# Making the low halves of streamed weights on VectorE instead of GpSimd

## The chip, the cores and the metric

The kernel runs on one core of a Trainium2 chip. A core has five engines that work side by side, each through its own queue in order: TensorE (PE; its weight loads are listed as PEld), VectorE (DVE), ScalarE (ACT), GpSimd (POOL) and SyncE (SP), which here issues the DMA transfers. The metric is the device time of one execution in microseconds (us); of several executions the median is given.

## The reference

One step of a decoder layer. A prompt of 2048 tokens and a small batch of 64 sample rows go through the same layer, of width 1024. In short:

```python
mod = jnp.einsum('bd,de->be', jax.nn.silu(c), w_ada) + b_ada     # six shifts, scales and gates
h = rms_norm(x, norm1_g) * (1 + sc1) + sh1
z = jnp.einsum('bld,de->ble', h, w_in)
q, k, v, g, u, gate_r, gate_s = jnp.split(z, IN_SPLITS, axis=-1)
ret = retention(rotary(q), rotary(k), v)     # then normalized, times silu(g)
ssm = s5(u, ...)                             # a complex diagonal scan, gelu, gated by w_glu
merged = sigmoid(gate_r) * (ret @ w_br) + sigmoid(gate_s) * (ssm @ w_bs)
x = x + gt1 * (merged @ w_out)
h2 = rms_norm(x, norm2_g) * (1 + sc2) + sh2
x = x + gt2 * (jnp.square(jax.nn.relu(h2 @ w_up)) @ w_down)
```

The outputs are the normalized rows of prompt and sample and the new states of both branches. All numbers are float32.

## The kernel before

The prompt is worked in four blocks of 512 tokens (`super_block`). After the four blocks comes one feed-forward stage (`feed_forward`) for all 2048 tokens, which has its own streams of weights and does not use the code of the change.

A float32 product is made of three products of a reduced type. Each operand is split: the high half is the value rounded to that type, the low half is what the rounding lost. PE then adds high times high, high times low and low times high in one PSUM bank (line 252, three matmuls per tile; 24 for one slice of weights against four banks).

The weights of the blocks come as one stream of slices of 128 x 2 x 512 numbers. The list of slices is laid down in `plan`: per block the matrices "u", "q", "k", "v", "g", four gate matrices, "glu", "br0", "br1", "bs0", "bs1", "wo0" and "wo1"; the first block also has eight matrices "ada4" to "ada11" of the modulation between them. The feed-forward of the 64 sample rows is worked on the side, with the matrices "us0" to "us7" in the third block and "ds0", "ds1" in the fourth, slice by slice between the others (`side`, line 226). There are 312 slices.

`fetch` (line 177) starts a slice's DMA into one of four raw buffers. `refill` (line 184) makes its two halves in one of five places of a ring: ACT rounds it into `whi` (line 190), and then the low half `wlo` is the difference of `wraw` and `whi` (line 193). After that the next fetch is issued; a fetch into a raw buffer waits on SP's queue until the low half of the slice that had it is made. A place of the ring comes free when PE has done its last product with it. In a block of the order "k" the refill for a used slice comes after the first bank's products of the next slice (lines 269 and 270); for "wo0" and "wo1" of the first three blocks, order "j", four refills come with the last bank.

What else uses the engines there: in the first block `s5_setup` (lines 933 to 1179) makes the tables of the scan, nearly all on DVE. In every block `s5` runs eight scan steps (lines 1206 to 1252), and `retention` four chunks (lines 1317 to 1359); both go back and forth between PE, DVE and ACT. DVE empties the banks of "q" and "k" (lines 1557 to 1559), of "v", "br", "bs" (lines 1699 and 1700) and "wo" (lines 1720 and 1721); ACT empties "u" and the gates. POOL makes further sums and low halves (lines 1347, 1560, 1649, 1702).

All these are generators that are stepped between groups of matmuls (`tick`), which lays down a program order. From this a planner, with its own assumed durations, sets the final order of each engine's queue ahead of time (line 1829); a tie to the program order is made where line 195 is called, for the first five slices. At run time every queue is worked in that fixed order.

Of the kernel before, what the change touches and what calls it, by code (L numbers as in the profile page):

```python
# [27 lines left out]
SIDE = ('us', 'ds')  # L28
# [53 lines left out]
class Layer:  # L82
# [101 lines left out]
    def refill(self, keep=False):  # L184
        nc = self.nc
        if self.split < len(self.stream):
            raw = self.rawq.pop(self.split)
            hi = self.ring.tile([P, 2, 512], F32R, name="whi")
            lo = self.ring.tile([P, 2, 512], F32R, name="wlo")
            a = nc.scalar.activation(hi, raw, AF.Copy)  # L190
            name = self.stream[self.split][0][:2]
            eng = nc.vector if name == "ad" or name in SIDE and self.split % 4 < 2 else nc.gpsimd
            l = eng.tensor_sub(lo, raw, hi)  # L193
            if keep:
                self.tc.keep_in_program_order(a)
                self.tc.keep_in_program_order(l)
            self.wq[self.split] = (hi, lo)
            self.split += 1
        self.fetch()
# [1641 lines left out]
```

## Time and profile before

| | |
|---|---|
| time, median of 3 runs (lowest to highest) | 3043.33 us (3043.03 to 3048.49) |
| the profiled execution | 3037.17 us |
| its span, first to last instruction | 3035.4 us |
| busy: PE, DVE, ACT, POOL | 2894.8, 1820.2, 1404.8, 1729.9 us |
| low halves made on POOL (line 193) | 248, busy 620.0 us |
| low halves made on DVE (line 193) | 64, busy 90.8 us |
| first and last low half start at | 40.7 and 1722.1 us |

In the profile's rows L193 is line 193 of the kernel, `wlo<-wraw,whi` says which tile is written from which, x248 is a count. In a list of groups, the numbers behind the bar are the busy time in us, the mean of one in ns, and the idle time of the engine just before them with what ended it. In a list of waits stand the waiting instruction, the one that ended the wait, the total in us, how often, and the longest. In a timeline the start in us and the duration come first; in the list of one source line the durations stand as shortest, median and longest in ns. PEclk is the share of TensorE's full clock that was granted.

### The profile page before, as it was taken

The numbers are of one execution on the slowest core, as the hardware profiler recorded it, in microseconds if no ns is written. First come the engines' busy times: TensorE is split into PE (matmuls) and PEld (weight loads), VectorE is DVE, ScalarE is ACT, GpSimd is POOL, SyncE is SP. The second block draws the span as 40 slices with busy tenths as digits, with TensorE's granted clock in tenths as the row PEclk, the third lists the DMA queues.
The fourth block names the chain that finished last, engine by engine and source line by source line (L and its number), as shares of the span: only waits on it lengthen the run. The fifth ranks groups of instructions, "written<-read, shape, count | busy, mean of one in ns | idle before, by whom it ended". The sixth has DMA issues, their size and how long they took to land.

```text
span 3035.4 us, 37377 instructions
## 1 busy us (share of the span) xinstructions
PE 2894.8 (95%) x13436; PEld 2371.7 (78%) x13436; DVE 1820.2 (60%) x2953; ACT 1404.8 (46%) x2280; POOL 1729.9 (57%) x1036
## 2 busy tenths in 40 slices
PE   8789999999999899999999999999999999999997
PEld 4568778788778788887788878887888788878886
DVE  6978544770676775365852655555556855555556
ACT  3223463322454334534344355555764555557743
POOL 3331355434354634565445677668777666679772
PEclk9889999999999999999999999999999999999998
DMA  8476435643236953447644555555544644457542
GB/s 264 140 210 196 131 128 175 184 119 119 82 100 211 280 172 114 144 161 229 191 132 146 179 179 185 185 200 203 180 160 160 211 167 153 154 203 248 190 153 98
DMA packets 337325, 518.62 MB, mean 171 GB/s; under 512 B 72038, under 2 KB 168822, under 8 KB 333035
## 3 DMA queue, kind: packets, MB, share of 16 engines
q1 hardware_dynamic: 337140, 516.24, 52.4%
q8 instruction: 106, 1.74, 0.2%
q14 instruction: 79, 0.65, 0.1%
HBM read 401.39 MB, written 114.78 MB: 170 GB/s over the span
## 4 chain that ended last, share of the span: by engine, by line
PE 75%; DVE 13%; DMA 4%; POOL 3%; ACT 2%; issue 2%; SPq 0%; ACTq 0%; DVEq 0%; POOLq 0%
PE pq_up L412 17%; PE pq_down L412 15%; PE pd_gr L252 6%; PE pd_wo L252 5%; PE pd_gs L252 5%; PE pd_br L252 3%; PE pd_u L252 2%; PE pd_g L252 2%; PE pd_bs L252 2%; PE pd_k L252 2%; PE pd_v L252 2%; PE pd_glu L252 2%; DMA sw<-sd 1%; POOL tw L310 1%; PE pd_q L252 1%
## 5 line engine op out<-in xcount | busy, mean ns | idle before, releaser
L193 POOL TENSOR_TENSOR wlo<-wraw,whi 128x1024 fp32r<-128x1024 f32 x248 | 620.0, 2512 | 701.0 <-ACT whi L190 582.9
L190 ACT ACTIVATE whi<-wraw 128x1024 fp32r<-128x1024 f32 x312 | 324.0, 1058 | 568.9 <-PE pd_wo L252 56.0
L412 PE MATMUL pq_down<-shi,tw 128*128 128x512 f32 x1792 | 561.1, 393 | 12.7 <-DVE acc L470 10.8
L412 PE MATMUL pq_up<-shi,tw 128*128 128x512 f32 x1776 | 552.6, 391 | 10.2 <-DVE tw L310 4.5
L412 PEld LDWEIGHTS pq_down<-shi,tw 128*128 128x128 f32 x1792 | 338.2, 189 | 85.4 <-ACT shi L399 7.9
L412 PEld LDWEIGHTS pq_up<-shi,tw 128*128 128x128 f32 x1776 | 334.6, 189 | 82.6 <-DVE tw L310 4.9
L310 POOL TENSOR_TENSOR tw<-traw,tw 128x512 fp32r<-128x512 f32 x191 | 280.5, 1482 | 150.9 <-ACT tw L309 150.5
L412 PE MATMUL pq_down<-slo,tw 128*128 128x512 f32 x896 | 351.0, 392 | 0.0
L412 PE MATMUL pq_up<-slo,tw 128*128 128x512 f32 x888 | 346.7, 391 | 0.0
L399 ACT ACTIVATE shi<-sw 128x1024 fp32r<-128x1024 f32 x140 | 146.9, 1057 | 159.3 <-DMA sw<-sd 109.6
L474 DVE SCALAR_TENSOR_TENSOR acc<-pq_down,modT,acc 128x512 f32<-128x512 f32 x224 | 161.7, 746 | 78.9 <-PE pq_down L412 78.5
L412 PEld LDWEIGHTS pq_down<-slo,tw 128*128 128x128 f32 x896 | 169.4, 189 | 34.4
L412 PEld LDWEIGHTS pq_up<-slo,tw 128*128 128x128 f32 x888 | 167.5, 189 | 34.5
L385 DVE TENSOR_TENSOR slo<-sw,far 128x512 fp32r<-128x512 f32 x160 | 104.2, 683 | 114.6 <-ACT far L384 102.8
L309 ACT ACTIVATE tw<-traw 128x512 fp32r<-128x512 f32 x223 | 136.7, 624 | 53.8 <-PE pq_down L412 37.3
L422 ACT ACTIVATE aq<-pq_up 128x512 f32<-128x512 f32 x128 | 72.5, 592 | 171.4 <-PE pq_up L412 171.4
L404 DVE TENSOR_TENSOR slo<-sw,shi 128x1024 fp32r<-128x1024 f32 x60 | 113.9, 1909 | 58.7 <-ACT shi L399 55.7
L193 DVE TENSOR_TENSOR wlo<-wraw,whi 128x1024 fp32r<-128x1024 f32 x64 | 90.8, 1421 | 72.2 <-ACT whi L190 67.7
L348 POOL TENSOR_TENSOR ts<-traw,ts 128x512 f32<-128x512 f32 x64 | 95.2, 1487 | 61.2 <-issue 51.2
L309 ACT ACTIVATE tw<-ts 128x512 fp32r<-128x512 f32 x127 | 79.5, 627 | 79.1 <-PE pq_up L412 72.2
L310 POOL TENSOR_TENSOR tw<-t,tw 128x512 fp32r<-128x512 f32 x64 | 88.1, 1385 | 35.3 <-ACT tw L309 35.3
L450 DVE TENSOR_TENSOR sq<-aq 128x512 f32<-128x512 f32 x32 | 29.6, 926 | 131.0 <-ACT aq L427 131.0
(546 smaller groups left out, 6939.8 us busy)
## 6 DMA issues: line engine op xcount, KB each, us to landing
wraw<-in_w_in_dram SPq DMA_DIRECT2D x144, 512.0 KB
sw<-sd SPq DMA_DIRECT2D x112, 512.0 KB
s5p<-s5c SPq DMA_DIRECT2D x32, 1024.0 KB
traw<-in_w_up_dram SPq DMA_DIRECT2D x64, 512.0 KB
sd<-sq SPq DMA_DIRECT2D x32, 1024.0 KB
sd<-aq SPq DMA_DIRECT2D x32, 768.0 KB
traw<-in_w_down_dram SPq DMA_DIRECT2D x24, 1024.0 KB
wraw<-in_w_ada_dram SPq DMA_DIRECT2D x32, 512.0 KB
```

The lines of the kernel that those rows point to most:

```text
L190: a = nc.scalar.activation(hi, raw, AF.Copy)
L193: l = eng.tensor_sub(lo, raw, hi)
L252: nc.tensor.matmul(banks[j], a, b, start=(k == 0 and z == 0), stop=(k == nk - 1 and z == 2))
L309: self.nc.scalar.activation(t[:, 0], x, AF.Copy)
L310: eng.tensor_sub(t[:, 1], x, t[:, 0])
L348: G.tensor_sub(x[p], l, x[m] if isinstance(m, int) else m)
L385: self.nc.vector.tensor_sub(d, a, c)
L399: nc.scalar.activation(hi[:, a], t, AF.Copy)
L404: V.tensor_sub(lo[:, a], t, hi[:, a])
L412: self.nc.tensor.matmul(bank, w, x, start=(first and a == 0 and z == 0), stop=(a == 3 and z == 2), skip_group_check=True)
L422: copy = lambda d, b: nc.scalar.activation(d, b, AF.Copy)
L474: V.scalar_tensor_tensor(d, b, g, d, op0=ALU.mult, op1=ALU.add)
```

## The change

Before, `refill` chose the engine of the subtraction by the name of the matrix: DVE for the "ada" matrices and for two of every four places of the side matrices "us" and "ds", POOL for all others. Now it is DVE for all 312. The subtraction's operands, the high half on ACT, the buffers and the fetches stay. The planner orders the queues anew.

```diff
             a = nc.scalar.activation(hi, raw, AF.Copy)
             name = self.stream[self.split][0][:2]
-            eng = nc.vector if name == "ad" or name in SIDE and self.split % 4 < 2 else nc.gpsimd
-            l = eng.tensor_sub(lo, raw, hi)
+            l = nc.vector.tensor_sub(lo, raw, hi)
             if keep:
                 self.tc.keep_in_program_order(a)
                 self.tc.keep_in_program_order(l)
```

## The prediction

> **What bounds the kernel now.** I read the page first, then the stretches of time, then the matrix engine's waits. Columns of the second fence: the stretch, its length, busy time and count of PE, PEld, DVE, ACT and POOL, then the granted PE clock, the DMA share and GB/s.
>
> ```profile
> span 3035.4 us, 37377 instructions
> PE 2894.8 (95%) x13436; PEld 2371.7 (78%) x13436; DVE 1820.2 (60%) x2953; ACT 1404.8 (46%) x2280; POOL 1729.9 (57%) x1036
> ```
>
> ```profile
> 0.00:503.00 503.00, 448.95 (x2098) 343.69 (x2099) 352.40 (x759) 188.51 (x292) 187.06 (x93) 0.95 0.56 177
> 0.00:1740.00 1740.00, 1642.09 (x7885) 1339.37 (x7886) 1070.50 (x2022) 678.44 (x1072) 808.40 (x384) 0.96 0.53 165
> 1740.00:3035.00 1295.00, 1252.71 (x5553) 1032.32 (x5551) 749.67 (x932) 726.41 (x1208) 921.47 (x652) 0.99 0.53 179
> 60.00:160.00 100.00, 78.30 (x348) 59.90 (x347) 98.01 (x248) 30.32 (x35) 38.54 (x18) 0.90 0.48 149
> 85.00:100.00 15.00, 9.44 (x33) 7.68 (x34) 14.65 (x74) 1.07 (x1) 0.00 (x0) 0.66 0.42 138
> ```
>
> PE is the bound: it is busy 95% of the span. The edited line works only in the four blocks, which end near 1740 us. There PE stands still for 1740 - 1642.1 = 97.9 us, and its clock is 0.96, so about 0.04 x 1642 = 66 us more go to the slower clock. DVE is busy 62% of the blocks, but 98% of 60 to 160 us, where the SSM tables are made: there DVE sets the pace. What PE waited for in the blocks (total, times, longest):
>
> ```profile
> PE py L1246 <- DVE s5t L1238: 13.9, 8, 5.2
> PE pd_k L252 <- DVE rt L1559: 11.7, 2, 10.2
> PE px L1217 <- issue: 10.4, 3, 6.5
> PE prt L1355 <- DVE rw L1351: 9.8, 3, 4.0
> PE pw L1159 <- DVE s5bx L1152: 8.0, 1, 8.0
> PE pt L917 <- DVE mt L911: 7.8, 1, 7.8
> PE pt L678 <- ACT xr L671: 5.2, 3, 2.2
> PE pms L766 <- DVE mS L1683: 5.1, 1, 5.1
> ```
>
> These eight are 71.9 us, 56.3 of them behind DVE. None names a low half. The row of the edited line says the same: in the list of those who waited for it, the matrix engine stands with 0.2 us.
>
> ```profile
> L193 POOL TENSOR_TENSOR wlo<-wraw,whi x248: 2339/2402/3972, 40.7 to 1722.1; 128x1024 fp32r<-128x1024 f32 x124
> L193 DVE TENSOR_TENSOR wlo<-wraw,whi x64: 1198/1223/3479, 63.1 to 1609.8; 128x1024 fp32r<-128x1024 f32 x64
> PEld pd_q L252: 0.2, 1
> ```
>
> So moving the low halves takes nothing off PE's path by itself. What counts is what it does to DVE, on which PE does wait.
>
> **The exchange on DVE.** Removed: 248 subtractions on POOL, median 2.40 us. Added: 248 on DVE, at the 1.22 us of the 64 that are there already: 248 x 1.22 = 303 us on an engine with 1740 - 1070.5 = 669.5 us idle. But the trace shows that a POOL subtraction also holds DVE up. First DVE, then POOL, in the stretch that DVE paces:
>
> ```profile
> 56.04 2.33 DVE L988 CAST s5w<-s5w 128x32 int32<-128x32 f32 x1
> 58.40 2.32 DVE L989 CAST s5w<-s5w 128x32 f32<-128x32 int32 x1
> ...
> 74.52 2.45 DVE L1036 TENSOR_SCALAR s5w<-s5w 128x64 f32<-128x64 f32 x1
> 77.02 2.38 DVE L1038 TENSOR_SCALAR s5w<-s5w 128x64 f32<-128x64 f32 x1
> 79.47 2.41 DVE L994 SCALAR_TENSOR_TENSOR s5w<-s5w 128x64 f32<-128x64 f32 x1
> 81.80 2.37 DVE L1036 TENSOR_SCALAR s5w<-s5w 128x64 f32<-128x64 f32 x1
> 84.74 0.18 DVE L1036 TENSOR_SCALAR s5w<-s5w 128x64 f32<-128x64 f32 x1
> ...
> 110.32 1.75 DVE L1147 TENSOR_TENSOR s5bx<-s5bc,s5pw 128x512 f32<-128x512 f32 x1
> 111.99 1.78 DVE L1148 TENSOR_TENSOR s5bx<-s5bc,s5pw 128x512 f32<-128x512 f32 x1
> 113.70 2.85 DVE L1150 TENSOR_TENSOR s5bx<-s5bc,s5pw 128x512 f32<-128x512 f32 x1
> 116.47 2.82 DVE L1147 TENSOR_TENSOR s5bx<-s5bc,s5pw 128x512 f32<-128x512 f32 x1
> 119.21 2.82 DVE L1148 TENSOR_TENSOR s5bx<-s5bc,s5pw 128x512 f32<-128x512 f32 x1
> 121.96 0.68 DVE L1150 TENSOR_TENSOR s5bx<-s5bc,s5pw 128x512 f32<-128x512 f32 x1
> ```
>
> ```profile
> 72.94 11.18 POOL L193 TENSOR_TENSOR wlo<-wraw,whi 128x1024 fp32r<-128x1024 f32 x4 [12.26 <-ACT whi L190]
> 113.18 8.30 POOL L193 TENSOR_TENSOR wlo<-wraw,whi 128x1024 fp32r<-128x1024 f32 x3
> ```
>
> An operation of 0.18 us takes 2.45 while POOL makes a low half, one of 0.68 takes 2.85: about 2.2 us, nearly one POOL subtraction, is lost per meeting. So where DVE is full, each low half costs it up to 2.2 us now and would cost 1.22.
>
> **The sum, part by part** (minus is faster).
>
> (1) The DVE-paced stretch. Taken away: the four at 74 to 84 us, 9.61 - 4 x 0.2 = 8.8; the five from 110 us, 12.02 - 5 x 0.68 = 8.6; the two casts, 4.65 - 2 x 0.18 = 4.3; together 21.7. Added: 13 low halves of 60 to 160 us (row below) and the two over the casts, 15 x 1.22 = 18.3. I take -3. Bounds: -22 if all the additions find holes, +16 if each also waits as in (5), 15 x 1.06.
>
> ```profile
> 60.00:160.00 100.00, 14.60 (x12) 30.79 (x13) 0.90 0.48 149
> ```
>
> (2) The ends of the blocks, where the merge after the branch products reads only SBUF.
>
> ```profile
> L1700 DVE TENSOR_TENSOR tb<-tb,gr 128x512 f32<-128x512 f32 x32 | 51.5, 1637 | 0.3
> ```
>
> The same operation on this shape, two SBUF inputs, took 0.68 us at 121.96 above: 32 x (1.637 - 0.68) = 30.6 us lie there, against four low halves per block for the two "bs" matrices, 16 x 1.22 = 19.5. PE's waits at these ends are pms and pt<-xr, 10.3 us. I take half of them, -5; bounds -10.3 and +10 (half the 19.5).
>
> (3) The scan steps and retention chunks (py, prt: 23.7 us of PE waits). A step's copy and subtraction of lines 1234 and 1238 are held up as well:
>
> ```profile
> L1238 DVE TENSOR_TENSOR s5t<-s5t 128x252 f32<-128x252 f32 x32 | 22.7, 710 | 0.4
> 1037.71 0.41 DVE L1238 TENSOR_TENSOR s5t<-s5t 128x252 f32<-128x252 f32 x1
> ```
>
> A step gets back 0.3 us here and like amounts on its other lines, and gets one or two low halves of 1.22 set between; the work is about even. But the order is fixed ahead, and an operation that takes now 0.18 and now 2.45 us can't be planned around; steadier times should spare a part of the waits. I take -3; bounds -23.7 and +9.8 (the 8 steps that PE waited for, 1.22 each).
>
> (4) Emptying the banks of "q" and "k", which DVE does alone: three operations per bank, read from PSUM.
>
> ```profile
> L1559 DVE TENSOR_TENSOR rt<-pd_k,rot 64x512 f32<-64x512 f32 x16 | 10.9, 683 | 0.2
> ```
>
> They take 0.68 to 0.69 us each time, so POOL never held them up and nothing comes back here. Twelve take 8.2 us per block, eight times; the next block needs the banks in turn, and a low half set among the twelve makes all behind it 1.22 us late: at most 8 x 1.22 = 9.8. I take half, +4, since a side or sample product gives PE other work at many of these places. Lower bound 0.
>
> (5) The new wait. A low half waits for its high half from ACT, and on DVE the bank emptying, the scan steps and the merges queue behind it, and PE behind those.
>
> ```profile
> DVE wlo L193 <- ACT whi L190: 67.7, 19, 12.4
> ```
>
> The 64 now there cost 67.7 / 64 = 1.06 us of DVE idling each; 248 more make 262 us, inside the 669.5 idle. No row of PE's waits has DVE's low half as cause. I take +2; the upper bound is rival B.
>
> (6) SP fetches the next raw tile when a low half is made, and its other loads queue behind that fetch.
>
> ```profile
> SPq L180 <- POOL wlo L193: 756.7, 194, 19.8
> ```
>
> A low half that takes 1.22 and not 2.40 us lets each fetch go 1.2 us sooner; PE's 10.4 us at px (a load for the scan) may shrink. I take -2; bounds -10.4 and +4 (a DVE low half that comes late holds the fetch).
>
> Sum: -3 - 5 - 3 + 4 + 2 - 2 = -7 us of PE waits. With each us waited goes 66 / 97.9 = 0.67 us of lost clock (85 to 100 us: 0.66 after PE's 7.8 us wait), so -7 x 1.67 = -12 us. Against the profiled execution, 3037.2 us (3035.4 span and 1.8 around it), that is 3025; the median shown is 3043.3, so the forecast is 3043 - 12 = 3031 us. After 1740 us nothing changes.
>
> [...]
>
> **The rivals.**
>
> A, no change: relief and additions cancel, which (1), (3) and (4) already do nearly; DVE's sum speaks for it. 3037 to 3049, say 3043.
>
> B, slower: low halves stand waiting for ACT in front of DVE's bank emptying. Place: the eight passages from "q" and "k" blocks; 1.5 low halves fall in each (8.2 us; a slice is 24 products of 1642.1 / 7885 = 0.21 us, 5 us). Price: 8 x 1.5 x (1.22 + 1.06) = 27 us; less the gains of (1), (2), (3) and (6), 13, it is +14, with the clock's 1.67 +23: 3066. It decides from about (13 + 3.6) / 12 = 1.4 us per low half, its own 1.22 and 0.2 of waiting. For it: the longest of the 19 waits is 12.4 us. Against it: those 64 low halves show in no wait of PE.
>
> C, much faster: the waits behind DVE (56.3 us) were mostly POOL's doing, and half of them vanish: 28 x 1.67 = -47, 2996. For it: the 2.2 us per meeting, in the very stretches where PE waits. Against it: the added 1.22.
>
> **How the numbers follow.** A median of this kernel tells about 0.2%, 6 us, from no change. Forecast (3018 to 3037): 0.34. C: 0.11. A: 0.25. B: 0.30. Faster 0.45, same 0.25, slower 0.30. The range leaves out the lower half of C and the upper part of B: 3006 to 3058.
>
> **What would show it.** DVE's group of line 193 becomes x312 near 1.22 us mean, POOL's goes; line 1700 falls towards 0.7 us, the operations of 74 to 84 us to 0.2; DVE in the blocks is busy near 1070 + 303 less the relief (62% becomes 65 to 75%). PE idles less than 97.9 us before the feed-forward, at a clock above 0.96. I am wrong by (4) and (5) if pd_k and pd_v waiting for line 1559, or for line 193 itself, come to over 20 us, and by (1) if 60 to 160 us has the same PE time as now. If the feed-forward's 1295 us move by more than 3, my claim that nothing changes there fails.

## The result and the profile after

The changed kernel takes 2989.06 us (median of 4 runs, 2987.39 to 2990.94), the kernel before 3043.18 us. The ratio is 0.9818, 95% interval 0.9806 to 0.983: 54 us faster. The forecast was 3031 us, with a range from 3006 to 3058 us. The time lies below the range, near the 2996 us of rival C.

In the changed kernel every line from 192 on has a number one lower, so its low half is L192, and L1237 there is L1238 of before. The experiments below keep the numbers of before. First the page of the changed kernel.

```profile
span 2989.2 us, 37370 instructions
PE 2881.5 (96%) x13436; PEld 2358.9 (79%) x13436; DVE 1890.0 (63%) x3201; ACT 1402.3 (47%) x2280; POOL 1123.8 (38%) x788
```

Next the stretches of time, with the columns of the prediction. The first product of the feed-forward starts at 1692.3 us, and in the kernel before at 1743.6. First the row of before cut at that place, then three rows of after.

```profile
0.00:1743.60 1743.60, 1645.69 (x7901) 1342.34 (x7902) 1074.03 (x2026) 678.44 (x1073) 810.05 (x386) 0.96 0.53 165
```

```profile
0.00:1692.30 1692.30, 1628.76 (x7901) 1328.07 (x7902) 1143.42 (x2274) 676.23 (x1072) 203.94 (x138) 0.98 0.54 170
1692.30:2989.20 1296.90, 1252.74 (x5537) 1030.86 (x5535) 746.62 (x928) 726.05 (x1208) 919.88 (x651) 0.98 0.53 177
60.00:160.00 100.00, 85.03 (x365) 63.43 (x364) 97.75 (x263) 30.86 (x35) 13.74 (x8) 0.88 0.47 150
```

The blocks are 51.3 us shorter. PE's idle time there fell from 1743.6 - 1645.7 = 97.9 to 63.5 us, 34.4 less, and the same 7901 products took 16.9 us less, at a granted clock of 0.98 and not 0.96. The feed-forward took 5.1 us more (1291.8 before). So the span of the profiled execution is 46.2 us shorter; the medians differ by 54. From 60 to 160 us, where DVE sets the pace, PE is busy 85.0 us and was 78.3.

DVE is the row to look at. It received 248 subtractions and is only 69 us busier. What it does itself, and what it waits for, in the changed kernel (groups of instructions; the last row is of the list of waits):

```profile
L192 DVE TENSOR_TENSOR wlo<-wraw,whi 128x1024 fp32r<-128x1024 f32 x312 | 386.8, 1252 | 210.1 <-ACT whi L190 169.5 <-PE ps_ds L225 14.7 <-PE ps_ada L257 12.3
L1699 DVE TENSOR_TENSOR tb<-tb,gr 128x512 f32<-128x512 f32 x32 | 26.3, 847 | 0.1
L1237 DVE TENSOR_TENSOR s5t<-s5t 128x252 f32<-128x252 f32 x32 | 13.3, 416 | 0.3
...
DVE wlo L192 <- ACT whi L190: 169.5, 103, 7.7
```

The low halves take 386.8 us against 90.8, 296 more; so all else on DVE takes 296 - 69 = 227 us less. The merge fell from 1637 to 847 ns, the scan's subtraction from 710 to 416. The stretch that DVE paces shows it one by one (timeline of DVE, after): the table operations that took 2.4 us each take 0.2, and the low halves stand between them.

```profile
75.90 0.18 DVE L1035 TENSOR_SCALAR s5w<-s5w 128x64 f32<-128x64 f32 x1
76.00 0.22 DVE L993 SCALAR_TENSOR_TENSOR s5w<-s5w 128x64 f32<-128x64 f32 x1
76.14 1.22 DVE L192 TENSOR_TENSOR wlo<-wraw,whi 128x1024 fp32r<-128x1024 f32 x1
77.28 0.19 DVE L1037 TENSOR_SCALAR s5w<-s5w 128x64 f32<-128x64 f32 x1
```

PE's waits in the blocks after (total, times, longest):

```profile
PE pd_k L251 <- DVE rt L1558: 9.2, 4, 6.0
PE pd_v L251 <- DVE rt L1558: 9.1, 5, 3.2
...
PE px L1216 <- issue: 5.0, 1, 5.0
PE pw L1158 <- DVE s5bx L1151: 4.6, 2, 3.9
PE pd_glu L251 <- ACT gh L1633: 4.2, 2, 3.2
PE pt L677 <- ACT xr L670: 3.9, 1, 3.9
PE pd_bs L251 <- DVE tb L1698: 3.8, 2, 1.9
...
PE py L1245 <- DVE s5t L1237: 2.5, 2, 1.3
```

The scan's wait (py) went from 13.9 to 2.5 us; the retention's (prt, 9.8), the modulation's (pt<-mt, 7.8) and the merge's (pms, 5.1) are gone from the list. Emptying "q" and "k" went from 11.7 and 4.1 to 9.2 and 9.1.

### The profile page after: what moved, and what is told of

Read it like the earlier page. It is cut to its first block, busy times and chain, and to the rows that moved or that the text cites. A ratio compares the mean times of both kernels' runs of the same rounds, so it can differ in the third digit from the quotient of the medians.

```text
span 2989.2 us, 37370 instructions
## 1 busy us (share of the span) xinstructions
PE 2881.5 (96%) x13436; PEld 2358.9 (79%) x13436; DVE 1890.0 (63%) x3201; ACT 1402.3 (47%) x2280; POOL 1123.8 (38%) x788
## 5 line engine op out<-in xcount | busy, mean ns | idle before, releaser
L192 DVE TENSOR_TENSOR wlo<-wraw,whi 128x1024 fp32r<-128x1024 f32 x312 | 386.8, 1252 | 210.1 <-ACT whi L190 169.5
L1346 POOL TENSOR_TENSOR R<-R,cpk 128x512 f32<-128x512 f32 x16 | 20.7, 1292 | 435.1 <-DVE R L1345 265.2
L403 DVE TENSOR_TENSOR slo<-sw,shi 128x1024 fp32r<-128x1024 f32 x60 | 104.3, 1754 | 53.3 <-ACT shi L398 49.3
L1559 POOL TENSOR_TENSOR qU<-qU,rt 128x512 f32<-128x512 f32 x16 | 24.2, 1512 | 244.4 <-DVE rt L1558 156.3
```

What stands on the lines that cost most here:

```text
L192: l = nc.vector.tensor_sub(lo, raw, hi)
L403: V.tensor_sub(lo[:, a], t, hi[:, a])
```

## The experiments

Three readings were put against each other. H: an instruction of GpSimd that reads SBUF holds VectorE up, and that was what PE waited for. S: the low halves are ready sooner and their raw buffers are fetched again sooner. O: the planner's new order is better by itself. Each run is given as the median and the ratio to the kernel before on the same chip, with its interval. The change itself stands at 0.9818. The edits are shown shortened; `(as before)` stands for the old condition.

**GpSimd reads again (echo5), and its control (after5).**

```diff
-        self.w2 = pool("w2", 6)
+        self.w2 = pool("w2", 5); self.scr = self.const.tile([P, 512], F32, name="scr")
...
+            eng = nc.vector
+            l = eng.tensor_sub(lo, raw, hi)
+            [nc.gpsimd.tensor_sub(self.scr, hi[:, z], hi[:, z]) for z in range(2)]   # echo5 alone, where GpSimd did it before
```

> All low halves on VectorE as in the change, and for each of the 248 moved ones GpSimd now makes two subtractions of 128x512 from the high half into a spare tile that nobody reads; to make room the small work pool has 5 tiles instead of 6. Theory H (the gain is that GpSimd no longer holds VectorE's operations up): VectorE has the additions and is held up again, so the gain goes and more: about 3043 to 3090 us, lines 1036 and 1700 back at their durations of before. Theory S (the gain is that a low half is ready 1.2 us sooner and its raw buffer is fetched again sooner): the low halves are as soon as in the change, about 2989 us, at most 3000. Theory O (the planner's new order of VectorE's queue is itself better): about 2989 us as well.

> The change with the small work pool of 5 tiles and the unused spare tile, without the extra GpSimd subtractions: the control of the run before. All theories: 2989 us, within 10.

Measured: echo5 3065.46 us, 1.0083 (1.0061 to 1.0106); after5 2993.06 us, 0.984 (0.9819 to 0.9861). Nothing reads the results of these extra subtractions, and they cost 72 us; the time lies where H had it. They do one thing besides: they keep the high half's place in the ring longer, and ACT waited 38.4 us in all for that. But PE stood idle 43 us longer than in after5 (111.4 against 68.0 us in the blocks), and its waits for a high or low half come to 7.5 us. In the blocks of echo5 DVE does the same 2274 instructions as in the change:

```profile
0.00:1768.80 1768.80, 1657.39 (x7901) 1343.27 (x7902) 1343.18 (x2274) 676.59 (x1072) 945.93 (x633) 0.96 0.53 163
```

It is busy 1343.2 and not 1143.4 us: 200 us of holding up. For the kernel before I had reckoned 201 us, by comparing each DVE operation that ran over a POOL low half with the shortest of its kind. That the two numbers agree is chance: 79 of the 200 lie on the low halves that DVE makes itself here (465.8 against 386.8 us). Line 1700 rose to 1072 ns, not back to 1637. S falls: it forecast 2989 us for low halves made as in the change. The scan's wait is back; in after5 the same row has 2.1 us. The timeline of DVE shows the hold's length, that of one GpSimd subtraction of 128x512 (1.50 us on the mean of 481):

```profile
PE py L1246 <- DVE s5t L1238: 11.7, 10, 3.4
```

```profile
130.53 1.53 DVE L1147 TENSOR_TENSOR s5bx<-s5bc,s5pw 128x512 f32<-128x512 f32 x1
131.98 1.52 DVE L1148 TENSOR_TENSOR s5bx<-s5bc,s5pw 128x512 f32<-128x512 f32 x1
```

**GpSimd writes without reading (memlo).**

```diff
-            l = eng.tensor_sub(lo, raw, hi)
+            l = eng.tensor_sub(lo, raw, hi) if eng is nc.vector else eng.memset(lo.bitcast(F32), 0.0)
```

> The kernel before, but GpSimd fills the 248 low halves with zeros instead of subtracting, so it reads nothing for them; the low parts of these weights are left out of the products. VectorE's work is that of before. Theory H: VectorE gets the relief (227 us of busy time) without the 296 us of additions, so it is as fast as the change or faster, 2960 to 2990 us. Theory O: VectorE's instructions are those of before and so is their order, so the time stays near 3043 us. Theory S: low halves are early here too, so 2989 us; this run can't tell H from S.

Measured: 2952.12 us, 0.971 (0.9686 to 0.9734). DVE keeps its instructions of before, and the blocks' row (first) shows it busy 864.8 us, where it was 1074.0. The second row is GpSimd's.

```profile
0.00:1656.00 1656.00, 1617.92 (x7901) 1322.72 (x7902) 864.83 (x2026) 677.37 (x1072) 420.31 (x386) 0.98 0.55 174
...
L193 POOL MEMSET wlo<- 128x1024 f32 x248 | 235.8, 961 | 910.0 <-PE pd_gr L252 96.1 <-PE pd_gs L252 88.1 <-PE ps_ds L226 82.4
```

O said that the time stays near 3043 with the work of before; it fell by 87 us against the kernel before beside it (3039.36 us), and below the 2960 us that H gave as its least. The orders were not quite the same, since the planner knows a fill from a subtraction. Against the change beside it (after5, 2993.06 us) memlo is 41 us faster. That is a rough size for what the 248 additions cost the change, and no bound: the fills are shorter and wait for no high half, and a fill still holds up some operations with one input (line 1038 takes 0.91 us here, 0.19 at its shortest):

```profile
71.84 3.74 POOL L193 MEMSET wlo<- 128x1024 f32 x4 [14.07 <-PE pd_u L252]
73.78 0.91 DVE L1038 TENSOR_SCALAR s5w<-s5w 128x64 f32<-128x64 f32 x1
```

Two operations with two SBUF inputs, which took up to 2.82 and 2.57 us before, stay within 0.04 us of their shortest time here:

```profile
L1147 DVE TENSOR_TENSOR s5bx<-s5bc,s5pw x8: 670/673/693, 93.7 to 169.1; 128x512 f32<-128x512 f32 x8
L1238 DVE TENSOR_TENSOR s5t<-s5t x32: 391/414/424, 207.3 to 1425.6; 128x252 f32<-128x252 f32 x32
```

**One input, and shorter pieces (cplo, pool4).**

```diff
# cplo
+            l = eng.tensor_sub(lo, raw, hi) if eng is nc.vector else eng.tensor_copy(lo, hi)
# pool4
+            l = eng.tensor_sub(lo, raw, hi) if eng is nc.vector or keep else [eng.tensor_sub(lo[:, z // 2, z % 2 * 256:z % 2 * 256 + 256], ...) for z in range(4)]   # raw and hi cut alike
```

> The kernel before, but GpSimd copies the high half into the low half instead of subtracting: one input read instead of two. The low halves of these weights are wrong by that, the work has the same shape. If a GpSimd instruction with one SBUF input holds VectorE up as well: by its length, 3000 to 3043 us, with small operations of VectorE at the copy's length again. If it takes two inputs to hold VectorE up: as with zeros filled in, 2945 to 2960 us.

> The kernel before, but each low half on GpSimd is made in four pieces of 128x256 (the first five slices are made on VectorE). If an operation of VectorE is held up until the GpSimd instruction that runs ends, a meeting costs at most a quarter, about 0.65 us, and part of the 201 us of holding up goes: 3005 to 3035 us. If the two engines only share bandwidth, the pieces change nothing: 3043 us.

Measured: cplo 2966.44 us, 0.9754 (0.974 to 0.9769); pool4 3012.68 us, 0.9909 (0.9892 to 0.9926). In pool4 the low halves of the first five slices that GpSimd made before stay whole on GpSimd, not on VectorE as expected: four, beside 244 in pieces. The time of cplo fits neither of its two forecasts, and its timeline shows why: a copy does hold DVE up, but only for its own 1.04 us. First cplo, then pool4 (DVE):

```profile
74.80 1.06 DVE L1039 SCALAR_TENSOR_TENSOR s5w<-s5w 128x64 f32<-128x64 f32 x1
75.78 1.07 DVE L999 SCALAR_TENSOR_TENSOR s5w<-s5w 128x64 f32<-128x64 f32 x1
```

```profile
75.79 0.76 DVE L994 SCALAR_TENSOR_TENSOR s5w<-s5w 128x64 f32<-128x64 f32 x1
76.47 0.74 DVE L1036 TENSOR_SCALAR s5w<-s5w 128x64 f32<-128x64 f32 x1
```

So in these runs the hold lasts about as long as the GpSimd instruction: 2.4 us before, where a subtraction took 2.40 (median), 1.5 in echo5, 1.05 here, 0.75 in pool4, where a piece took 0.74. In pool4 there are more meetings, each shorter, and the sum is smaller. pool4 also answers a fourth reading, that GpSimd's other work comes sooner when its queue is shorter: up to 1690 us GpSimd is busy 953.3 us there and 771.7 before, and the kernel is faster all the same.

**How many (half, b0).**

```diff
# half
+            eng = nc.vector if (as before) or self.split % 2 else nc.gpsimd
# b0
+            eng = nc.vector if (as before) or self.split < 86 else nc.gpsimd
```

> Every second one of the moved low halves on VectorE, the other half on GpSimd as before. Theory H: the holding up goes with the number left on GpSimd, so about half the gain, 3008 to 3025 us. Theory O: the order is new here too, so anything from 2989 to 3043 us, with no relation to the number.

> Only the 86 slices of the first block on VectorE, the rest as before. Theory H with a local effect: the first block shortens by about 25 us as it did in the change (455 to 430 us), the others keep their lengths of before: 3015 to 3020 us. My prediction's view (the gain lies only where VectorE is full, that is in 60 to 160 us of the first block): the first block alone would give nearly all of the gain, about 2995 us. Theory O: no relation.

Measured: half 3016.61 us, 0.992 (0.9894 to 0.9946); b0 3017.68 us, 0.9919 (0.9891 to 0.9947). In half 140 of the 248 stay on GpSimd, and the 108 that moved give 44% of the gain. In b0 54 moved; the first block is 431.9 us long, against 455.5 before and 430.1 in the change, and the others stay within 3 us of before (446.9, 408.7, 389.3). So the first block holds nearly half of the gain and the other three the rest; the view that nearly all lies in the stretch that DVE fills falls.

**Where (qkv_pool, gates_pool, late_pool, gates0, mix).** Each leaves some of the 248 on GpSimd:

```diff
# qkv_pool
+            eng = nc.gpsimd if self.stream[self.split][0] in ("q", "k", "v") else nc.vector
# gates_pool;  gates0: ... and self.split < 86
+            eng = nc.gpsimd if name in ("gr", "gs") else nc.vector
# late_pool;  mix: ... and self.split >= 86
+            eng = nc.gpsimd if name in ("gr", "gs", "gl", "br", "bs", "wo") else nc.vector
```

> The change, but the 48 low halves of the matrices q, k and v stay on GpSimd. Term (4) of my prediction (a low half among the bank emptyings of q and k costs 1.22 us each time): faster than the change by up to 9.8 us and the clock's share, about 2977 to 2985 us, with less waiting of PE for line 1559. Theory H: these slices fall where the scan steps fill VectorE, so their share of the gain is lost, 48/248 of 54 us or more: 2999 us or above. Theory S: 2999 us.

> The change, but the 64 low halves of the four gate matrices of each block stay on GpSimd. If each low half on GpSimd costs the same wherever it lies: 64/248 of 54 us, 3003 us. If the place decides (in the gates ScalarE empties the banks and VectorE is little used, only the retention chunks run there): 2987 to 2997 us, much less per low half than the 25 us that 48 low halves of q, k and v cost.

> The low halves of everything after g (gates, glu, br, bs, wo: 136 of the 248) stay on GpSimd; those of u, q, k, v, g, the ada matrices and the side matrices are on VectorE. If each low half counts the same: 136/248 of 54 us lost, 3019 us. If the place decides: only retention chunks and the merges of line 1700 are held up again, 10 to 20 us of PE waits and their clock at most, 2995 to 3012 us.

| run | low halves left on GpSimd | median us | ratio (interval) | length of the four blocks, us |
|---|---|---|---|---|
| the change | 0 | 2989.06 | 0.9818 (0.9806 to 0.983) | 430, 443, 393, 378 |
| qkv_pool | 48 | 3013.69 | 0.9912 (0.9894 to 0.9931) | 437, 445, 404, 387 |
| gates_pool | 64 | 3000.61 | 0.9865 (0.9843 to 0.9886) | 443, 449, 394, 376 |
| late_pool | 136 | 2989.44 | 0.9825 (0.9807 to 0.9842) | 445, 437, 395, 375 |
| gates0 | 16 | 3003.68 | 0.987 (0.9852 to 0.9887) | 443, 447, 393, 376 |
| mix | 102 | 2995.76 | 0.9839 (0.9824 to 0.9854) | 432, 449, 397, 375 |

With 48 of 248 on GpSimd, qkv_pool loses about half of the gain, and PE's wait for the scan (py) is back at 10.6 us; late_pool has 136 there and takes no longer than the change as a whole. So the number does not decide. But gates_pool (3001 us) and late_pool (2989 us) fit neither of their forecasts, and late_pool holds all that gates_pool leaves on GpSimd: its first block is 15 us longer than in the change, and its other blocks and the feed-forward are 11 us shorter in the profiled execution. These matrices differ by what runs with them: in the last three blocks PE does the scan steps' products during "k" to "g", in the first from "g" into the gates. That made the question for the next two runs.

> The change, but the 16 low halves of the first block's gates stay on GpSimd. In the first block alone the scan steps run during the gates. If the place decides, these 16 cost as much as all 64 gate slices did: the first block at 443 instead of 430 us, 2998 to 3004 us. If the planner's order made that cost: 2985 to 2995 us.

> The first block all on VectorE as in the change; in the other three blocks gr, gs, glu, br, bs and wo on GpSimd, u, q, k, v, g and the side matrices on VectorE. If the place decides, the first block has the length it had in the change (430 us, against 445 with its late part on GpSimd) and the others those of the run with the late part on GpSimd (437 + 395 + 375 us): 2989 - 15 = 2975 us, faster than both kernels. If the differences of about 10 us between such variants are the planner's order alone: 2985 to 3000 us.

gates0 came out as the place says: 16 low halves bring the whole 13 us of gates_pool's first block, and the scan's wait with them. The first block is 442 to 445 us long in the three runs that leave these 16 on GpSimd, and 429 to 434 us in the six that leave none or almost none there (the change, after5, b0, mix, mlsl, all_dve). PE's waits in the first block of gates0:

```profile
PE py L1246 <- DVE s5t L1238: 4.7, 2, 4.1
...
PE prt L1355 <- DVE rw L1351: 2.1, 1, 2.1
```

In the change neither stands among the waits of that block. mix has the first block as forecast (432), but missed its 2975 us and came out where the planner's order alone was to put it (2985 to 3000 us): its second block is 449 us long and not 437. The second block goes from 437 to 449 us among these runs with no relation to what stays on GpSimd. What in the planner's order makes these 10 us is left open; a single difference of that size between two variants shows nothing about H.

**More off GpSimd (mlsl, all_dve).**

```diff
# both
-            nc.gpsimd.tensor_sub(sl[:, j], t, sh[:, j])
+            V.tensor_sub(sl[:, j], t, sh[:, j])
-                nc.gpsimd.tensor_sub(ml[d][:, j], t, mh[d][:, j])
+                V.tensor_sub(ml[d][:, j], t, mh[d][:, j])
# all_dve
-                nc.gpsimd.tensor_add(dst[:, j], dst[:, j], t)
+                V.tensor_add(dst[:, j], dst[:, j], t)
-            nc.gpsimd.tensor_mul(R, R, c[:, C_G128:C_G128 + H, None].to_broadcast([P, H, P]))
+            V.tensor_mul(R, R, c[:, C_G128:C_G128 + H, None].to_broadcast([P, H, P]))
```

> The change, and the 48 low halves of the merge and of the gated scan output (lines 1649 and 1702) on VectorE too. Theory H: 54 us of holding up remain in the blocks in the change, about 20 of them at these lines; they go, and 48 x 0.68 = 33 us of work come: 2980 to 2995 us, no change that can be told.

> As the run before, and the sums of the rotated q and k (line 1560) and the decay of the retention state (line 1347) on VectorE too, so that GpSimd does almost nothing in the blocks. Theory H alone: the last 54 us of holding up go, 2980 to 2990 us. Term (4) of my prediction: the emptying of a bank of q and k becomes 2.7 instead of 2.06 us on VectorE, 4 x 0.68 = 2.7 us later at each of 8 passages, so +22 us and the clock's share: 3000 to 3025 us.

Measured: mlsl 2995.55 us, 0.9841 (0.9818 to 0.9865); all_dve 2999.15 us, 0.9854 (0.9832 to 0.9877). mlsl is within what the planner's order does. all_dve is 10 us slower than the change by the medians and lies between its two forecasts, 1 us below that of term (4). The 22 us that term (4) made of the longer bank emptying did not come: PE's waits at pd_k and pd_v are 13.7 us there and 18.3 in the change, while pd_g waiting for vU went from 1.7 to 7.9. No variant that makes every low half beat the change.

## Why the prediction was wrong

The mechanism was in it: POOL's low halves hold DVE up by about their own length (2.2 us a meeting, at 2.40 us each), PE waits on DVE and not on low halves (56.3 us in the eight rows, and 0.2), and with the waiting goes clock besides (34.4 us less idle, 16.9 us less for the same products). The sizes were wrong, and most of all that of one term.

- **Term (3), the scan steps and retention chunks: the step that failed.** I took -3 us on the ground that a step's relief and its added low halves are "about even"; py and prt came from 23.7 to 2.5, -21.2, close to the lower bound of -23.7. As a sum "about even" holds, and even in time: from the first to the last operation of a step on DVE (lines 1224 to 1238) it is 9.3 us on the mean before and 9.6 in the change, with 56 low halves begun inside the 32 steps. But PE does not wait for the length of a step. It waits where a step ends later than the place that the fixed order gave to PE's next product. What I had written down, that an operation of now 0.18 and now 2.45 us can't be planned around, fits that, and I let it spare 3 of 23.7 us. qkv_pool (10.6 us of py again), echo5 (11.7) and gates0 (4.7) show that GpSimd's reads bring these waits. That a plan kept more closely is what spares them was not tested by itself, and the length of one hold does not give the size: in pool4, with holds of 0.75 us, py is 14.7 us.
- **Term (1), the table stretch:** taken -3; the waits pt<-mt and pw went from 15.8 to 4.6, -11.2. I had counted the eleven held operations that I showed and left the others at nothing, while I charged all fifteen low halves.
- **Term (2), the ends of the blocks:** taken -5, measured near 0. pms and pt<-xr fell from 10.3 to 3.9, but pd_bs (3.8, new) and pd_glu (1.4 to 4.2) came in their place. The merge itself lost its hold as said.
- **Term (4), emptying "q" and "k":** taken +4; pd_k and pd_v went from 15.8 to 18.3, +2.5. The number is near by luck. In the change only one low half starts inside the eight passages, so what the term counted hardly happened. qkv_pool has 18.7 us at these rows and is slower. And "nothing comes back here" was wrong: in memlo, without the subtractions, the same rows have 1.9 us.
- **Term (5), the new wait:** 248 more were to idle DVE by 262 us; it waits 169.5 us in all, 0.54 and not 1.06 us each. Line 192 stands with 0.5 us in PE's waits. Rival B had 12 low halves standing in the eight passages; one does.
- **Term (6), the loads for the scan:** taken -2; the rows of px together went from 13.3 to 10.8, -2.5.
- **The sum:** as measured the six terms give -11.2 + 0.2 - 21.2 + 2.5 + 0.5 - 2.5 = -31.7 us, of the 34.4 us by which PE's idle time fell; the forecast had -7.
- **The clock:** 0.67 us for each us waited was assumed; 16.9 / 34.4 = 0.49 was measured.
- **The feed-forward** was to stay within 3 us and became 5.1 us longer in the profiled execution. That claim failed; in the other runs it lies between 1291.5 and 1298.6, so I make nothing of it.

Rival C had the right place and nearly the right time, with a chance of 0.11. The 56.3 us of PE waits behind DVE, in the same eight rows, fell to 16.3; over all rows of PE's waits behind DVE it is 78 and 44 us. C had said that 28 us go. What I set against it, "the added 1.22", was the mistake of term (3) once more.

## What to carry to other kernels

When an engine's short operations take, now and then, as long as one instruction of a neighbour, add up this excess over the shortest of each kind before costing a move: here it was 201 us against 296 us of moved work, and the move paid. Weigh it where the critical engine waits for work that goes back and forth, such as the scan steps: 16 low halves beside them in the first block cost it 13 us, while the 102 of the later matrices in the other three blocks left these 6 us shorter in one run (late_pool) and 7 us longer in another (mix), no more than the planner's order does. A sum of busy time does not tell this.

## What the runs showed of the hardware

- GpSimd's subtractions and copies, which read SBUF, held up VectorE operations with two SBUF inputs (line 1147: 0.68 us, up to 2.82 before), and scalar operations and casts with one (line 1036: 0.18 and 2.45; line 988: 2.33), by about the length of the GpSimd instruction: 2.4, 1.5, 1.05 and 0.75 us. I had not expected that a one-input copy does it too (1.05 us in cplo), nor that a fill of 0.96 us does so little: in memlo DVE's busy time in the blocks is 209 us less than before (864.8 against 1074.0). In the stretch from 72 to 76 us of memlo the operations held beside fills begin with one source (lines 1036 and 1038: 0.90 to 1.57 us, 0.19 else); the others that show it (0.66 to 1.47 us) start 0.10 to 0.24 us behind such a one and end with it. Lines 1147 and 1238 have none there.
- In the record of both traces the granted clock is either full or half, and in the blocks each stretch at half lasts one to five times 3.41 us:

```
before: 16 stretches at 0.5, 122.9 us in all (3.41 to 17.07 us each)
after:  11 stretches at 0.5,  75.1 us in all (3.41 to 13.65 us each)
```

Of the 16 stretches before, nine follow a gap of PE of 3.7 to 10.2 us, six one of 1.5 to 2.9 us, and one follows none over 1 us; of the 11 after, five follow gaps of 3.6 to 6.0 us, five gaps of 1.2 to 3.2 us and one none. Gaps over 3.41 us, the one before PE's first product among them, fell from 10 to 6, and the same products took 16.9 us less; a stretch lasted 7.7 us on the mean before, 3.8 us of lost time (an estimate, half of 7.7).
